# A batched f32 matmul with subtraction: x loaded as f16 through GpSimd's DMA queue into a ring of slots

## The chip, the cores and the metric

The kernel runs on one core of a Trainium2 chip. The metric is the device time of one execution in microseconds (us). The times shown are those of several executions of the kernel, with their median; one further execution was recorded by the hardware profiler and gives the profile and the trace.

A core has five engines with a queue of instructions each: TensorE (PE; its weight loads are listed apart as PEld), VectorE (DVE), ScalarE (ACT), GpSimd (POOL) and SyncE (SP). Transfers between the chip's DRAM and the core's memory (SBUF) are issued from such a queue and carried out by 16 DMA engines.

## The reference

```python
def setup_inputs():
    batch, m, k, n = 16, 512, 1024, 768
    return {
        "x": np.random.randn(batch, m, k).astype(np.float32),
        "weight": np.random.randn(k, n).astype(np.float32),
        "sub_value": np.random.randn(batch, m, n).astype(np.float32),
    }

def reference(x, weight, sub_value):
    return (np.matmul(x, weight) - sub_value).astype(np.float32)
```

Batch and m together are 8192 rows. x holds 33.55 MB, sub_value and the output 25.17 MB each, and weight 3.15 MB: 87.04 MB that must cross between DRAM and SBUF at least once.

## The kernel before

The 8192 rows are worked as 64 m tiles of 128 rows. Eight m tiles form a block whose rows are dealt so that each of the 128 partitions holds eight neighbouring rows of DRAM; a transfer of n neighbouring tiles therefore reads n rows in one piece for each partition (4 KB of x and 3 KB of sub_value or output per row).

For an m tile the steps are these. Its x rows, f32, are loaded (`load_x`, issued at L87). ScalarE casts them to f16 (`cast`, L108, or L105 for the tiles in `ON_DVE`). TensorE needs x with k on the partitions, so the tile is transposed. For 50 tiles TensorE does it, four times 128x128 words of 32 bits, each word a pair of f16 values (L116), into `psum_t`, and ScalarE copies the result to `xt_tile` (L123). For the 14 tiles of `ON_DVE`, taken in pairs, VectorE does it with 16 block transposes a pair (L137) into `xtp_tile`. Sixteen matmuls of 128x384 follow (L149): four chunks c of k, two interleaved halves r of each chunk, two halves of n. They accumulate in `psum_o`, of which there are three buffers. VectorE then subtracts (`finish`, L160): it reads `psum_o` and the tile of sub_value and writes the result over the latter. The output is stored from there (`store`, L97).

The weight comes in four chunks (L79) that pass through buffers of the sub_value pool and are cast to f16 by VectorE (L81).

All transfers are issued from SP in program order. The first 20 are listed in `HEAD_TRANSFERS`: single x tiles alternate with weight chunks, then single tiles of x and sub_value alternate, then pairs. From m tile 3 on the main loop issues, at every fourth tile, a group of four x tiles three groups ahead, a group of four sub_value tiles two groups ahead, and the store of the group two groups back. x has four buffers of four tiles, sub_value with output seven.

Every instruction is kept in program order on its engine (`keep`). In the main loop, TensorE's order is: the matmuls of chunk c of tile mi, then a transpose of tile mi + 2, and so on for four chunks. ScalarE casts four tiles ahead (seven for pairs of `ON_DVE`). At the start TensorE runs matmuls on zeros (`idle`) in the gaps while the first x tiles and the weight arrive; tiles 0 to 2 are multiplied chunk by chunk as the weight comes in.

Of the kernel before, what the change touches and what calls it, by code (L numbers as in the profile page):

```python
# [8 lines left out]
P = 128  # L9
Q = 32  # L10
F32 = mybir.dt.float32
F16 = mybir.dt.float16

S = 8
G = 4
XA, SA, OA = 3, 2, 2
TA = 2
CA = 2
LEAD_DVE = 7
PER = 4  # L20
HEAD = 3
ON_DVE = frozenset(range(18, 60, 6))
HEAD_TRANSFERS = [('x', 0, 1), ('w', 0, 0), ('x', 1, 1), ('w', 1, 0), ('x', 2, 1), ('w', 2, 0), ('w', 3, 0), ('x', 3, 1), ('s', 0, 1), ('x', 4, 1), ('s', 1, 1), ('x', 5, 1), ('s', 2, 1), ('x', 6, 1), ('s', 3, 1), ('x', 7, 1), ('x', 8, 2), ('s', 4, 2), ('x', 10, 2), ('s', 6, 2)]


@with_exitstack
def kernel(
# [7 lines left out]
    nc = tc.nc  # L35
    keep = tc.keep_in_program_order
# [5 lines left out]
    M_TOT, K = x_flat.shape  # L42
    _, N = weight.shape
    n_mt = M_TOT // P
    n_g = n_mt // G
    NS = N // 2
    KW = K // 2
    n_c = KW // P

    x_s = x_flat.rearrange("(s p j) k -> s p j k", p=P, j=S)  # L50
    sub_s = sub_flat.rearrange("(s p j) n -> s p j n", p=P, j=S)
    out_s = out_flat.rearrange("(s p j) n -> s p j n", p=P, j=S)
    w_c = weight.rearrange("(c p r) n -> c p r n", p=P, r=2)

    def rows(view, mi, n):
        return view[mi // S][:, mi % S : mi % S + n]

    const_pool = ctx.enter_context(tc.tile_pool(name="const", bufs=1))
    w_pool = ctx.enter_context(tc.tile_pool(name="w_pool", bufs=1))
    x_pool = ctx.enter_context(tc.tile_pool(name="x_pool", bufs=4))  # L60
    x16_pool = ctx.enter_context(tc.tile_pool(name="x16_pool", bufs=CA + 2))
    xt_pool = ctx.enter_context(tc.tile_pool(name="xt_pool", bufs=TA + 3))
    x16p_pool = ctx.enter_context(tc.tile_pool(name="x16p_pool", bufs=2))
    xtp_pool = ctx.enter_context(tc.tile_pool(name="xtp_pool", bufs=2))
    so_pool = ctx.enter_context(tc.tile_pool(name="so_pool", bufs=7))
    psum_t_pool = ctx.enter_context(tc.tile_pool(name="psum_t", bufs=2, space=bass.MemoryType.PSUM))
    psum_o_pool = ctx.enter_context(tc.tile_pool(name="psum_o", bufs=3, space=bass.MemoryType.PSUM))

# [3 lines left out]

    w_sb = w_pool.tile([P, n_c, 2, N], F16)

    x_t, so_t, x16_t, xt_t, ps_t, po_t = {}, {}, {}, {}, {}, {}

    def load_w(c):
        st = so_pool.tile([P, 2, N], F32, name="w_stage", tag="so_tile")
        keep(nc.sync.dma_start(out=st, in_=w_c[c]))  # L79
        for r in range(2):  # L80
            keep(nc.vector.tensor_copy(out=w_sb[:, c, r], in_=st[:, r]))  # L81

    def load_x(mi, n):
        g, j = divmod(mi, G)
        if j == 0:
            x_t[g] = x_pool.tile([P, G, K], F32, name="x_tile")
        keep(nc.sync.dma_start(out=x_t[g][:, j : j + n], in_=rows(x_s, mi, n)))  # L87

    def load_sub(mi, n):
        g, j = divmod(mi, G)  # L90
        if j == 0:
            so_t[g] = so_pool.tile([P, G, N], F32, name="so_tile")
        keep(nc.sync.dma_start(out=so_t[g][:, j : j + n], in_=rows(sub_s, mi, n)))

    def store(mi, n):
        g, j = divmod(mi, G)
        keep(nc.sync.dma_start(out=rows(out_s, mi, n), in_=so_t[g][:, j : j + n]))  # L97

    def cast(mi):
        g, j = divmod(mi, G)  # L100
        first = mi - mi % 2
        if first in ON_DVE:
            if mi == first:
                x16_t["pair", mi] = x16p_pool.tile([P, 2, K], F16, name="x16p_tile")
            keep(nc.scalar.copy(out=x16_t["pair", first][:, mi - first], in_=x_t[g][:, j]))  # L105
            return
        x16_t[mi] = x16_pool.tile([P, K], F16, name="x16_tile")
        keep(nc.scalar.copy(out=x16_t[mi], in_=x_t[g][:, j]))  # L108


    def transposes(mi):
        def one(c):
            def f():
                if c == 0:
                    ps_t[mi] = psum_t_pool.tile([P, K], F16, name="psum_t")
                keep(nc.tensor.transpose(  # L116
                    ps_t[mi].bitcast(F32)[:, c * P : (c + 1) * P],
                    x16_t[mi].bitcast(F32)[:, c * P : (c + 1) * P],
                    ident,
                ))  # L120
                if c == n_c - 1:
                    xt_t[mi] = xt_pool.tile([P, K], F16, name="xt_tile")
                    keep(nc.scalar.copy(out=xt_t[mi], in_=ps_t.pop(mi)))  # L123
                    x16_t.pop(mi)
            return f
        return [one(c) for c in range(n_c)]

    def transposes_dve(mi):

        x16 = x16_t.pop(("pair", mi)).bitcast(F32).rearrange("p j (c q) -> p (j c) q", c=n_c)  # L130
        xt_p = xtp_pool.tile([P, 2, K], F16, name="xtp_tile")
        xt_t[mi], xt_t[mi + 1] = xt_p[:, 0], xt_p[:, 1]
        xt = xt_p.bitcast(F32).rearrange("p j (c m) -> p (j c) m", c=n_c)

        def one(a, b):
            def f():
                keep(nc.vector.transpose(  # L137
                    xt[b * Q : (b + 1) * Q, :, a * Q : (a + 1) * Q],
                    x16[a * Q : (a + 1) * Q, :, b * Q : (b + 1) * Q],
                ))  # L140
            return f
        return [one(a, b) for a in range(P // Q) for b in range(P // Q)]

    def matmuls(mi, c):
        if c == 0:
            po_t[mi] = psum_o_pool.tile([P, 2, 512], F32, name="psum_o")
        for r in range(2):
            for h in range(2):
                keep(nc.tensor.matmul(  # L149
                    po_t[mi][:, h, :NS],  # L150
                    xt_t[mi][:, 2 * P * c + r : 2 * P * (c + 1) : 2],
                    w_sb[:, c, r, h * NS : (h + 1) * NS],
                    start=(c == 0 and r == 0),
                    stop=(c == n_c - 1 and r == 1),
                ))

    def finish(mi):
        g, j = divmod(mi, G)
        o = so_t[g][:, j].rearrange("p (h n) -> p h n", h=2)
        keep(nc.vector.tensor_tensor(  # L160
            out=o, in0=po_t.pop(mi)[:, :, :NS], in1=o, op=mybir.AluOpType.subtract
        ))


    for kind, at, n in HEAD_TRANSFERS:
        {"w": lambda: load_w(at), "x": lambda: load_x(at, n), "s": lambda: load_sub(at, n)}[kind]()


    idle_w = const_pool.tile([P, P], F16)
# [5 lines left out]
    def idle(n):  # L175
        for _ in range(n):
            keep(nc.tensor.matmul(idle_o[:, 0], idle_w, idle_x, start=True, stop=True))  # L177

    def lead(mi):
        return LEAD_DVE if mi - mi % 2 in ON_DVE else TA + CA  # L180

    def transpose_tile(mi):
        for f in transposes(mi):
            f()

    idle(13)
    cast(0)
    transpose_tile(0)
    idle(5)
    matmuls(0, 0)  # L190
    cast(1)
    transpose_tile(1)
    idle(4)
    matmuls(0, 1)
    matmuls(1, 0)
    matmuls(1, 1)
    cast(2)
    transpose_tile(2)
    idle(3)
    matmuls(0, 2)  # L200
    matmuls(1, 2)
    for c in range(3):
        matmuls(2, c)
    cast(3)
    transpose_tile(3)
    for mi in range(HEAD):
        matmuls(mi, 3)
        finish(mi)
    for mi in range(HEAD + 1, HEAD + TA):
        cast(mi)  # L210
        transpose_tile(mi)
    for mi in range(HEAD + TA, n_mt):
        if mi - lead(mi) < HEAD:
            cast(mi)


    waiting = []
    for mi in range(HEAD, n_mt):
        g, j = divmod(mi, G)
        if j == 0 or mi == HEAD:  # L220
            if g + XA < n_g:
                load_x((g + XA) * G, G)
            if g + SA < n_g:
                load_sub((g + SA) * G, G)
            if g >= OA:
                store((g - OA) * G, G)
        t = mi + TA
        tr = transposes(t) if t < n_mt and t - t % 2 not in ON_DVE else []
        for c in range(n_c):
            matmuls(mi, c)  # L230
            if tr:
                tr[c]()
        for t in range(mi, n_mt):
            if t - lead(t) == mi:
                cast(t)
        finish(mi)
        if mi + LEAD_DVE - 1 in ON_DVE:
            waiting += transposes_dve(mi + LEAD_DVE - 1)
        for f in waiting[:PER]:
            f()  # L240
        del waiting[:PER]
    for g in range(n_g - OA, n_g - 1):
        store(g * G, G)
    store(n_mt - G, G - 2)
    store(n_mt - 2, 1)
    store(n_mt - 1, 1)


# [28 lines left out]
```

## Time and profile before

| what | value |
|---|---|
| median of 8 executions | 213.08 us (212.73 to 213.47) |
| the profiled execution, its own time | 212.74 us |
| the profiled execution, span from the first to the last instruction | 211.0 us |
| granted TensorE clock, mean | 0.992 of full speed |
| DMA, mean over the span | 413 GB/s |
| L160, the subtraction | 64 times, 957 ns each |
| L123, the copy of a transposed tile | 50 times, 1012 ns each |
| L108 and L105, the casts of x | 50 times 1048 ns and 14 times 1046 ns |
| L137, VectorE's transposes | 112 times, 436 ns each |

The span lies within the execution's own time; 1.74 us of that execution are outside it. In the profile a line L123 is line 123 of the kernel. A group of instructions is shown as line, engine, operation, output <- input, shape and count, then the busy time in us, the mean of one in ns, and the idle time of the engine just before them with what ended most of it. In the row PEclk and the row DMA each digit is a tenth of full clock, or of the DMA engines' time, in one of 40 equal slices of the span. A line of the timeline or of the chain of waits starts with the start in us and the duration in us. A line of the windows has the stretch in us, its length, then busy time and count of instructions for PE, PEld, DVE, ACT and POOL, then the granted clock, the share of DMA time and GB/s.

### The profile page before, as it was taken

The page shows a single profiled execution, that of the slowest core. Times are in us where ns is not written, and L with a number is a line of the kernel's source. Part 1 is how long each engine was busy: PE and PEld are TensorE (multiplying, and loading weights), DVE is VectorE, ACT ScalarE, POOL GpSimd, SP SyncE. Part 2 cuts the span into 40 slices and gives each one's busy share as a digit, 9 for nine tenths or more (in the row PEclk, how much of TensorE's full clock was granted, in tenths as well). Part 3 has the DMA queues.
Part 4 walks back from the last instruction along what each step waited for, and adds up shares of the span by engine and source line. Part 5 has one row for each costly group of instructions (what it writes and reads, how often), then busy time and mean ns, then how long its engine had stood idle before and what let it go on. Part 6 is the DMA issues. An engine that isn't in the chain of part 4 may idle for free.

```text
span 211.0 us, 3028 instructions
## 1 busy us (share of the span) xinstructions
PE 198.5 (94%) x1249; PEld 130.0 (62%) x1249; DVE 114.0 (54%) x186; ACT 112.6 (53%) x115; POOL 0.7 (0%) x6
## 2 busy tenths in 40 slices
PE   7999799999999999999989999997999999999970
PEld 2465566677666666666656577664656766766640
DVE  0343313152597299389519939940993995133330
ACT  3646666757842847465086555508655552567300
POOL 1000000000000000000000000000000000000000
PEclk9999999999999999999999999999999999999996
DMA  6999999999999999999999999999999999999994
GB/s 225 423 409 400 419 418 430 440 415 432 425 416 433 424 422 430 444 415 434 419 431 426 425 436 411 435 422 428 434 423 434 418 436 423 422 426 424 433 409 170
DMA packets 9374, 87.23 MB, mean 413 GB/s; under 512 B 1040, under 2 KB 1040, under 8 KB 3728
## 3 DMA queue, kind: packets, MB, share of 16 engines
q1 hardware_dynamic: 9360, 87.04, 98.3%
q8 instruction: 10, 0.16, 0.3%
q14 instruction: 4, 0.03, 0.0%
HBM read 61.87 MB, written 25.17 MB: 413 GB/s over the span
## 4 chain that ended last, share of the span: by engine, by line
DMA 49%; PE 33%; ACT 9%; DVE 3%; SPq 1%; issue 1%; ACTq 0%
DMA x_tile<-in_x_dram 49%; PE psum_o L149 28%; PE psum_t L116 5%; ACT x_tile L108 4%; ACT xt_tile L123 3%; ACT x16p_tile L105 2%; DVE xtp_tile L137 2%; DVE so_tile L160 1%; SPq L79 1%; SPq L87 1%; ACTq L105 0%
## 5 line engine op out<-in xcount | busy, mean ns | idle before, releaser
L149 PE MATMUL psum_o<-w_sb,xt_tile 128*128 128x384 f16 x800 | 145.9, 326 | 2.1 <-ACT xt_tile L123 2.1
L149 PEld LDWEIGHTS <-xt_tile 128*128 128x128 f16 x800 | 78.2, 98 | 42.2 <-ACT xt_tile L123 3.2
L160 DVE TENSOR_TENSOR so_tile<-psum_o,so_tile 128x768 f32<-128x768 f32 x64 | 60.7, 957 | 57.3 <-PE psum_o L149 39.5
L123 ACT COPY xt_tile<-psum_t 128x1024 f16<-128x1024 f16 x50 | 50.6, 1012 | 59.7 <-PE psum_t L116 59.0
L137 DVE STREAM_TRANSPOSE xtp_tile<-x16p_tile 32x256 f32<-32x256 f32 x112 | 48.8, 436 | 22.8 <-ACT x16p_tile L105 21.0
L108 ACT CAST x_tile<-x_tile 128x1024 f16<-128x1024 f32 x50 | 51.7, 1048 | 6.7 <-DMA x_tile<-in_x_dram 6.7
L116 PE MATMUL psum_t<-ident,x_tile 128*128 128x128 f32 x200 | 52.4, 274 | 1.9 <-ACT x_tile L108 1.4
L149 PE MATMUL psum_o<-w_sb,xtp_tile 128*128 128x384 f16 x224 | 42.9, 326 | 0.6 <-DVE xtp_tile L137 0.6
L116 PEld LDWEIGHTS psum_t<-ident,x_tile 128*128 128x128 f32 x200 | 27.6, 141 | 16.0 <-ACT x_tile L108 4.3
L149 PEld LDWEIGHTS <-xtp_tile 128*128 128x128 f16 x224 | 21.8, 98 | 10.9 <-DVE xtp_tile L137 1.4
L105 ACT CAST x16p_tile<-x_tile 128x1024 f16<-128x1024 f32 x14 | 14.6, 1046 | 20.6 <-DMA x_tile<-in_x_dram 20.6
L81 DVE CAST w_sb<-w_stage 128x768 f16<-128x768 f32 x8 | 4.1, 556 | 10.5 <-DMA w_stage<-in_weight_dram 10.5
L177 PE MATMUL psum_o<-idle_x,idle_w 128*128 128x512 f16 x25 | 8.4, 491 | 1.3 <-DVE idle_x L172 1.3
L177 PEld LDWEIGHTS <-idle_w 128*128 128x128 f16 x25 | 3.1, 122 | 4.9 <-issue 3.2
L108 ACT ACT_TABLE_LOAD x1 | 1.3, 1283 | 0.7 <-PEq L261 0.7
L171 DVE MEMSET idle_w<- 128x64 uint32 x1 | 0.1, 112 | 0.8 <-PEq L261 0.8
masks.py:199 POOL TENSOR_SCALAR_AFFINE_SELECT ident<-ident 128x128 f32<-128x128 f32 x1 | 0.3, 292 | 0.1
L172 DVE MEMSET idle_x<- 128x256 uint32 x1 | 0.3, 272 | 0.0
masks.py:197 POOL MEMSET ident<- 128x128 f32 x1 | 0.2, 204 | 0.3 <-POOLq L261 0.3
L261 POOL MEMSET const-bfloat16-1.0<- 128x1 bf16 x1 | 0.1, 101 | 0.0
L261 POOL MEMSET const-uint8-127<- 128x1 uint8 x1 | 0.1, 101 | 0.0
L261 POOL MEMSET const-float32-0.0<- 128x1 f32 x1 | 0.1, 99 | 0.2 <-issue 0.2
(1 smaller groups left out, 0.1 us busy)
## 6 DMA issues: line engine op xcount, KB each, us to landing
x_tile<-in_x_dram SPq DMA_DIRECT2D x13, 2048.0 KB, 31.0
out_dram<-so_tile SPq DMA_DIRECT2D x15, 1536.0 KB, 31.9
so_tile<-in_sub_value_dram SPq DMA_DIRECT2D x14, 1536.0 KB, 33.1
x_tile<-in_x_dram SPq DMA_DIRECT2D x8, 512.0 KB, 10.5
w_stage<-in_weight_dram SPq DMA_DIRECT2D x4, 768.0 KB, 8.6
x_tile<-in_x_dram SPq DMA_DIRECT2D x2, 1024.0 KB, 12.8
so_tile<-in_sub_value_dram SPq DMA_DIRECT2D x4, 384.0 KB, 11.0
so_tile<-in_sub_value_dram SPq DMA_DIRECT2D x2, 768.0 KB, 13.4
```

Of the source, the lines that this page charges most:

```text
L79: keep(nc.sync.dma_start(out=st, in_=w_c[c]))
L81: keep(nc.vector.tensor_copy(out=w_sb[:, c, r], in_=st[:, r]))
L87: keep(nc.sync.dma_start(out=x_t[g][:, j : j + n], in_=rows(x_s, mi, n)))
L105: keep(nc.scalar.copy(out=x16_t["pair", first][:, mi - first], in_=x_t[g][:, j]))
L108: keep(nc.scalar.copy(out=x16_t[mi], in_=x_t[g][:, j]))
L116: keep(nc.tensor.transpose(ps_t[mi].bitcast(F32)[:, c * P : (c + 1) * P], x16_t[mi].bitcast(F32)[:, c * P : (c + 1) * P], ident,))
L123: keep(nc.scalar.copy(out=xt_t[mi], in_=ps_t.pop(mi)))
L137: keep(nc.vector.transpose(xt[b * Q : (b + 1) * Q, :, a * Q : (a + 1) * Q], x16[a * Q : (a + 1) * Q, :, b * Q : (b + 1) * Q],))
L149: keep(nc.tensor.matmul(po_t[mi][:, h, :NS], xt_t[mi][:, 2 * P * c + r : 2 * P * (c + 1) : 2], w_sb[:, c, r, h * NS : (h + 1) * NS], start ...
L160: keep(nc.vector.tensor_tensor(out=o, in0=po_t.pop(mi)[:, :, :NS], in1=o, op=mybir.AluOpType.subtract))
L177: keep(nc.tensor.matmul(idle_o[:, 0], idle_w, idle_x, start=True, stop=True))
L261: nc = _bacc.Bacc("TRN2", target_bir_lowering=False, num_devices=1)
```

## The change

The x buffers become one ring of 32 slots, one m tile of f16 each (`x_ring`). The buffers of sub_value and output become one ring of 32 slots of f32 (`so_ring`); the four weight chunks pass through its last eight slots. Transfers are listed by hand in `TRANSFERS`, one list for GpSimd's queue and one for SP's, and take up to eight m tiles each. GpSimd's queue has all of x: tiles 0 to 3 singly, tiles 4 to 7 together, then eight at a time. As source and destination differ in type, the DMA casts x to f16 on its way. SP's queue has the weight, then sub_value for tiles 0 to 15, and then alternately the store of a block of eight tiles and the load of the block of sub_value sixteen tiles further on.

`issue` is called whenever a tile of x has been read, or a tile of output finished. It emits the next transfers of each list as long as the slots that they need have been freed by earlier instructions; the order in each queue is that of its list. ScalarE's casts and their buffers are gone. TensorE's and VectorE's transposes read `x_ring` directly. The order of the work on TensorE and VectorE, the idle matmuls at the start, the transposed tiles' buffers and those of PSUM are as before. In the changed kernel the transposes of TensorE stand at L134, the copies at L141, VectorE's transposes at L157, and the subtraction at L184.

```diff
-G = 4
-XA, SA, OA = 3, 2, 2
+NX, NSO = 32, 32
-CA = 2
-HEAD_TRANSFERS = [('x', 0, 1), ('w', 0, 0), ('x', 1, 1), ('w', 1, 0), ('x', 2, 1), ('w', 2, 0), ('w', 3, 0), ('x', 3, 1), ('s', 0, 1), ('x', 4, 1), ('s', 1, 1), ('x', 5, 1), ('s', 2, 1), ('x', 6, 1), ('s', 3, 1), ('x', 7, 1), ('x', 8, 2), ('s', 4, 2), ('x', 10, 2), ('s', 6, 2)]
+
+TRANSFERS = {"pool": [
+    ('x', 0, 1), ('x', 1, 1), ('x', 2, 1), ('x', 3, 1), ('x', 4, 4), ('x', 8, 8),
+    ('x', 16, 8), ('x', 24, 8), ('x', 32, 8), ('x', 40, 8), ('x', 48, 8), ('x', 56, 8),
+], "sp": [
+    ('w', 0, 1), ('w', 1, 1), ('w', 2, 1), ('w', 3, 1), ('s', 0, 4), ('s', 4, 4),
+    ('s', 8, 8), ('o', 0, 8), ('s', 16, 8), ('o', 8, 8), ('s', 24, 8), ('o', 16, 8),
+    ('s', 32, 8), ('o', 24, 8), ('s', 40, 8), ('o', 32, 8), ('s', 48, 8), ('o', 40, 8),
+    ('s', 56, 8), ('o', 48, 8), ('o', 56, 4), ('o', 60, 2), ('o', 62, 1), ('o', 63, 1),
+]}
...
-    x_pool = ctx.enter_context(tc.tile_pool(name="x_pool", bufs=4))
-    x16_pool = ctx.enter_context(tc.tile_pool(name="x16_pool", bufs=CA + 2))
+    x_pool = ctx.enter_context(tc.tile_pool(name="x_pool", bufs=1))
...
-    so_pool = ctx.enter_context(tc.tile_pool(name="so_pool", bufs=7))
+    so_pool = ctx.enter_context(tc.tile_pool(name="so_pool", bufs=1))
...
+    x_ring = x_pool.tile([P, NX, K], F16)
+    so_ring = so_pool.tile([P, NSO, N], F32)
+    todo = {q: list(t) for q, t in TRANSFERS.items()}
+    done = {"w": set(), "x": set(), "s": set(), "o": set(), "read": set(), "finish": set()}
+
+    def issue():
+        for queue in todo.values():
+            issue_from(queue)
+
+    def issue_from(todo):
+        while todo:
+            kind, at, n = todo[0]
+            span = set(range(at, at + n))
+            old = {t - NX if kind == "x" else t - NSO for t in span}
+            need, by = {
+                "w": (set(), "o"),
+                "x": ({t for t in old if t >= 0}, "read"),
+                "s": ({t for t in old if t >= 0}, "o"),
+                "o": (span, "finish"),
+            }[kind]
+            if not need <= done[by]:
+                return
+            todo.pop(0)
+            done[kind] |= span
...
+            here = ring[:, at % size : at % size + n]
+            there = view[at // S][:, at % S : at % S + n]
+            if kind == "x":
+                keep(nc.gpsimd.dma_start(out=here, in_=there))
+            elif kind == "o":
+                keep(nc.sync.dma_start(out=there, in_=here))
+            else:
+                keep(nc.sync.dma_start(out=here, in_=there))
...
-                    x16_t[mi].bitcast(F32)[:, c * P : (c + 1) * P],
+                    x_ring[:, mi % NX].bitcast(F32)[:, c * P : (c + 1) * P],
...
+                    done["read"].add(mi)
+                    issue()
...
-        x16 = x16_t.pop(("pair", mi)).bitcast(F32).rearrange("p j (c q) -> p (j c) q", c=n_c)
+        x16 = x_ring[:, mi % NX : mi % NX + 2].bitcast(F32).rearrange("p j (c q) -> p (j c) q", c=n_c)
...
-        if j == 0 or mi == HEAD:
-            if g + XA < n_g:
-                load_x((g + XA) * G, G)
-            if g + SA < n_g:
-                load_sub((g + SA) * G, G)
-            if g >= OA:
-                store((g - OA) * G, G)
...
-        for t in range(mi, n_mt):
-            if t - lead(t) == mi:
-                cast(t)
```

More of the change, by code (lines that the diff above doesn't have):

```diff
@@ L44 @@
     n_mt = M_TOT // P
-    n_g = n_mt // G
     NS = N // 2
@@ L59 @@
     w_pool = ctx.enter_context(tc.tile_pool(name="w_pool", bufs=1))
-    x_pool = ctx.enter_context(tc.tile_pool(name="x_pool", bufs=4))
-    x16_pool = ctx.enter_context(tc.tile_pool(name="x16_pool", bufs=CA + 2))
+    x_pool = ctx.enter_context(tc.tile_pool(name="x_pool", bufs=1))
     xt_pool = ctx.enter_context(tc.tile_pool(name="xt_pool", bufs=TA + 3))
-    x16p_pool = ctx.enter_context(tc.tile_pool(name="x16p_pool", bufs=2))
     xtp_pool = ctx.enter_context(tc.tile_pool(name="xtp_pool", bufs=2))
-    so_pool = ctx.enter_context(tc.tile_pool(name="so_pool", bufs=7))
+    so_pool = ctx.enter_context(tc.tile_pool(name="so_pool", bufs=1))
     psum_t_pool = ctx.enter_context(tc.tile_pool(name="psum_t", bufs=2, space=bass.MemoryType.PSUM))
@@ L73 @@
     w_sb = w_pool.tile([P, n_c, 2, N], F16)
[L75 to L108, printed above, removed]
+    x_ring = x_pool.tile([P, NX, K], F16)
@@ new lines @@
+    so_ring = so_pool.tile([P, NSO, N], F32)
+    xt_t, ps_t, po_t = {}, {}, {}
+    todo = {q: list(t) for q, t in TRANSFERS.items()}
[18 more added lines that the diff above has]
+            done[kind] |= span
+            if kind == "w":
+                first = NSO - 2 * (n_c - at)
+                st = so_ring[:, first : first + 2]
+                keep(nc.sync.dma_start(out=st, in_=w_c[at]))
+                for r in range(2):
+                    keep(nc.vector.tensor_copy(out=w_sb[:, at, r], in_=st[:, r]))
+                continue
+            ring, size, view = {
+                "x": (x_ring, NX, x_s), "s": (so_ring, NSO, sub_s), "o": (so_ring, NSO, out_s)
+            }[kind]
+            here = ring[:, at % size : at % size + n]
[6 more added lines that the diff above has]
+                keep(nc.sync.dma_start(out=here, in_=there))
@@ L114, in f @@
                 if c == 0:
+                    assert mi in done["x"]
                     ps_t[mi] = psum_t_pool.tile([P, K], F16, name="psum_t")
@@ L123, in f @@
                     keep(nc.scalar.copy(out=xt_t[mi], in_=ps_t.pop(mi)))
-                    x16_t.pop(mi)
+                    done["read"].add(mi)
+                    issue()
             return f
@@ L128, in transposes_dve @@
     def transposes_dve(mi):
-        x16 = x16_t.pop(("pair", mi)).bitcast(F32).rearrange("p j (c q) -> p (j c) q", c=n_c)
+        assert {mi, mi + 1} <= done["x"]
+        x16 = x_ring[:, mi % NX : mi % NX + 2].bitcast(F32).rearrange("p j (c q) -> p (j c) q", c=n_c)
         xt_p = xtp_pool.tile([P, 2, K], F16, name="xtp_tile")
@@ L140, in f @@
                 ))
+                if a == b == P // Q - 1:
+                    done["read"] |= {mi, mi + 1}
+                    issue()
             return f
@@ L157, in finish @@
     def finish(mi):
-        g, j = divmod(mi, G)
-        o = so_t[g][:, j].rearrange("p (h n) -> p h n", h=2)
+        assert mi in done["s"]
+        done["finish"].add(mi)
+        o = so_ring[:, mi % NSO].rearrange("p (h n) -> p h n", h=2)
         keep(nc.vector.tensor_tensor(
@@ L162, in finish @@
         ))
-    for kind, at, n in HEAD_TRANSFERS:
-        {"w": lambda: load_w(at), "x": lambda: load_x(at, n), "s": lambda: load_sub(at, n)}[kind]()
+        issue()
+    issue()
     idle_w = const_pool.tile([P, P], F16)
@@ L177, in idle @@
             keep(nc.tensor.matmul(idle_o[:, 0], idle_w, idle_x, start=True, stop=True))
-    def lead(mi):
-        return LEAD_DVE if mi - mi % 2 in ON_DVE else TA + CA
     def transpose_tile(mi):
@@ L186 @@
     idle(13)
-    cast(0)
     transpose_tile(0)
@@ L190 @@
     matmuls(0, 0)
-    cast(1)
     transpose_tile(1)
@@ L196 @@
     matmuls(1, 1)
-    cast(2)
     transpose_tile(2)
@@ L203 @@
         matmuls(2, c)
-    cast(3)
     transpose_tile(3)
@@ L209 @@
     for mi in range(HEAD + 1, HEAD + TA):
-        cast(mi)
         transpose_tile(mi)
-    for mi in range(HEAD + TA, n_mt):
-        if mi - lead(mi) < HEAD:
-            cast(mi)
     waiting = []
     for mi in range(HEAD, n_mt):
-        g, j = divmod(mi, G)
-        if j == 0 or mi == HEAD:
-            if g + XA < n_g:
-                load_x((g + XA) * G, G)
-            if g + SA < n_g:
-                load_sub((g + SA) * G, G)
-            if g >= OA:
-                store((g - OA) * G, G)
         t = mi + TA
@@ L241 @@
         del waiting[:PER]
[L242 to L246, printed above, removed]
+    assert not any(todo.values())
 _INS = ['x', 'weight', 'sub_value']
```

## The prediction

> **What bounds the kernel now.** I read the busy times first, then the 40 slices and the DMA queues, then the waits, and last the timeline of the start and the chain of waits. The page:
>
> ```profile
> PE 198.5 (94%) x1249; PEld 130.0 (62%) x1249; DVE 114.0 (54%) x186; ACT 112.6 (53%) x115; POOL 0.7 (0%) x6
> PEclk9999999999999999999999999999999999999996
> DMA  6999999999999999999999999999999999999994
> q1 hardware_dynamic: 9360, 87.04, 98.3%
> L149 PE MATMUL psum_o<-w_sb,xt_tile 128*128 128x384 f16 x800 | 145.9, 326 | 2.1 <-ACT xt_tile L123 2.1
> ```
>
> Two resources are full at once. The DMA engines are busy 98.3% of 211.0 us with 87.04 MB, all from one queue, and TensorE is busy 94% of it. ScalarE and VectorE have half their time free.
>
> The rate of TensorE can be read off the chain of waits, where it runs freely; stretches of three windows follow it:
>
> ```profile
> 31.11 0.11 PE psum_t L116
> 31.22 0.65 PE psum_o L149 x4
> 31.87 0.11 PE psum_t L116
> 31.98 0.65 PE psum_o L149 x4
> ```
> ```profile
> 0.00:31.87 31.87, 28.88 (x159) 16.75 (x160) 9.38 (x16) 17.98 (x18) 0.70 (x6) 1.00 0.96 383
> 31.87:204.45 172.58, 169.63 (x1093) 113.28 (x1090) 103.70 (x170) 94.60 (x98) 0.00 (x0) 1.00 1.01 427
> 204.45:211.00 6.55, 0.00 (x0) 0.00 (x0) 0.96 (x1) 0.00 (x0) 0.00 (x0) 0.72 0.52 213
> ```
>
> Four matmuls and one transpose come every 0.76 us, so a tile takes 4 x 0.76 = 3.04 us, and 4 x 0.65 = 2.6 us where VectorE transposes. With 50 tiles of the first kind and 14 of the second that is 188.4 us, 2.95 us a tile. From 31.87 us to the last matmul at 204.45 us TensorE stands still only 172.58 - 169.63 = 2.95 us. The DMA in that window moves 427 GB/s. An m tile is 0.524 MB of x, 0.393 MB of sub and 0.393 MB of out, 1.31 MB or 3.07 us: the same as TensorE's. So any lateness of TensorE in the start is kept to the end, and any DMA byte that becomes dearer lengthens the kernel.
>
> The timeline of the start shows when the first loads are used:
>
> ```profile
> 6.57 1.03 DVE L81 CAST w_sb<-w_stage 128x768 f16<-128x768 f32 x2 [5.36 <-DMA w_stage<-in_weight_dram]
> 14.76 1.03 DVE L81 CAST w_sb<-w_stage 128x768 f16<-128x768 f32 x2 [0.86 <-DMA w_stage<-in_weight_dram]
> 16.04 1.04 ACT L108 CAST x_tile<-x_tile 128x1024 f16<-128x1024 f32 x1 [1.98 <-DMA x_tile<-in_x_dram]
> ```
>
> The transfers are listed x0, w0, x1, w1, x2, w2, w3, x3, with 0.524 MB for an x tile and 0.786 MB for a w chunk. w0 has landed after 1.31 MB, w3 after 4.72, x3 after 5.24: (16.04 - 6.57) / (5.24 - 1.31) = 2.41 us per MB (0.415 MB/us), from 3.4 us on. What is listed first lands first. The transposes of tiles 5, 6, 7 and 8 begin at 22.54, 25.80, 28.84 and 31.87 us in the chain, each right behind the matmuls before it: x is in time there, because tiles 4 to 7 are single transfers and 8 to 11 pairs.
>
> **What the Trainium skill says.** "DMA: Bandwidth & Descriptors", section "SWDGE vs HWDGE vs iDMA": a cast in a DMA can be had only from GpSimd; "Issuing engines are not separate DMA queues": both queues run on the same 16 DMA engines. So a second queue gives no bandwidth; the trace agrees in so far as one queue fills them. The same page, "Queues, rings and completion order": a DMA engine takes the queues in turn, packet by packet. No run shows it yet. "SBUF — State Buffer", section "SBUF: two separate sides": a VectorE operation that uses its second port pair keeps GpSimd from writing descriptors. The candidates are eight w casts (L81, 4.1 us in all), so at most 4.1 us of descriptor writing, early. No page prices a cast.
>
> **The change part by part.**
>
> 1. ScalarE's casts go: 50 x 1.048 + 14 x 1.046 = 67 us of an engine at 53%. TensorE's waits for the cast copy are 4.3 + 1.4 us, mostly in the first 22 us, and after 31.87 us it loses 2.95 us, to late copies on ScalarE and late VectorE transposes behind it. I count 2.4 us gained: 0.70 + 0.30 + 1.38 at 108, 120 and 145 us, where the timeline has a wait for L123 or L137. At most 4 us, with a cast's delay in the start.
>
> 2. The x bytes. DMA reads the same 33.55 MB of f32 and writes half. Before, reads and writes of a transfer are equal in size, so the trace can't say which side binds. If the write side does, an x byte costs 0.5; if the read side, 1; if the cast has a rate of its own, more, and 2 is the upper bound that I keep. I take 1: every byte must still be read through engines that stand at 427 GB/s. Total then 87.04 / 0.427 = 204 us, as before: no gain and no loss in capacity.
>
> 3. The start. x4 to x7 become one transfer, x8 to x15 one of 4.19 MB, with one completion each; the changed program lets tile 8's first transpose wait for the whole of it. SP's queue holds w and sub 0 to 15 (9.44 MB) in the same time, with nothing to hold it back, as its first wait is that of the store of tiles 0 to 7, for L184 of tile 7. x8 to x15 are there when 8.39 MB of x are. If the queues share equally, 16.8 MB must move: 3.4 + 16.8 / 0.426 = 42.8 us. If SP's packets win (a sub row is up to 24 KB in one piece, a row of an x tile 4 KB), 17.8 MB: 45.3 us. I take 44.0 us against 31.87 us: TensorE stops for what adds up to **12.1 us**. Lateness ahead of it (x4 to x7, sub 0 to 3) is covered by this one, as TensorE waits for tile 8 anyway. So is GpSimd's issue: x0 comes behind the identity's 0.3 us (masks.py:199) and, by the skill's page ("Specifications"), some 0.4 us later to its first byte than on SP.
>
> 4. The middle. On SP the load of sub i+16 stands behind the store of tiles i to i+7, which waits for L184 of tile i+7; a pair is 6.29 MB and must be done in 8 x 2.95 = 23.6 us. x stays issued without a break: 25.2 MB remain at 44 us, and the ring is not full before its end. With equal shares SP gets 0.213 MB/us and a pair takes 29.5 us. From tile 7's finish at 44.0 + 6.6 = 50.6 us, subs 16, 24, 32 land at 80.1, 109.6, 139.1; they are needed at 77.2, 100.8, 124.4 by L184, plus 4.9 us that two spare psum_o buffers give: 3.9 us lost at tile 24, another 5.9 at tile 32; then x is through (156 us) and SP has all. Sum 9.8. If SP's packets win, x is the late one: a cycle of eight tiles is 10.48 MB, 24.6 us against 23.6, six cycles, 6 us. I take **8 us**; bounds 0 (a share just between) and 14 (x has 0.6).
>
> 5. The end: the last two stores are unchanged, so the 6.55 us behind the last matmul stay. SP's 65 issues, some 0.42 us each in the start's timeline (1.16 us: w0), become 24, with 12 on GpSimd, hidden beside transfers on both sides.
>
> Sum: +12.1 - 2.4 + 8 = +17.7 us. Against the profiled execution (212.74 us, 1.74 around the span of 211.0) 230.4; against the median of 213.08, 230.8. **I forecast 231 us.**
>
> **The rivals.**
>
> A. *The cast halves x's cost in the DMA.* For it: the writes halve. Against: reads don't. Total 70.3 MB, 165 us, so TensorE alone bounds. Place: the start. With x at 0.4 of the engines' time, x8 to x15 are there at 3.4 + 4.19 / 0.4 / 0.42 = 28.3 us, in time, and sub 0 to 3 at 3.4 + 4.72 / 0.6 / 0.42 = 22.1, some 1.2 us late for the psum_o buffer of tile 3. 213.1 + 1.2 - 2.4 = 211.9, with the cast's delay in the start gone about 211: not slower. It decides from an x byte at about 0.6 downward: at 0.7, 5.87 / 0.4 / 0.42 puts x8 at 38.3 us and 6 us are lost. With equal shares at 0.5 sub 0 to 3 come at about 26 us and the kernel is at 216.
>
> B. *The cast is slow in the DMA.* For it: the conversion is work the engines don't do now, and x comes in 2 KB rows per tile. Against: nothing in the trace. At 1.5 the load is 103.8 MB-equivalents: 3.4 + 103.8 / 0.427 = 246.5, with the last tiles and the end 255 us; at 2, 120.6 and 295 us.
>
> C. *One long stall only.* The shares fall so that the middle costs nothing: 213.1 + 12.1 - 2.4 = 223 us. It differs from the forecast only in step 4.
>
> That the rings make false waits is a rival that I drop: the changed program's waits are per transfer and per tile.
>
> **How the numbers follow.** Forecast (x byte at 0.9 to 1.15; 225 to 240 us) 0.47; C 0.12; B 0.28; A 0.13, of which 0.08 ends below the time before, 0.02 at it and 0.03 above. The range: A's slower part and its loss at 0.7 sit near 216, so it starts there; B reaches it up to about 1.55, so I end at 266. Outside stay about 0.1 below and 0.1 above. What can be told from no change is about 0.2%, 0.4 us. Faster 0.08, same 0.02, slower 0.90.
>
> **What would show it.** Step 3: L134 on TensorE with one wait of about 10 us or more for the DMA into x_ring before 46 us. Step 4: L184 idle for the DMA of sub near tiles 24 and 32, or L134 for x at each eighth tile. Step 2: GpSimd's queue with about 38% of the engines' time; a far larger share means B, about 24% means A. The forecast is wrong if x8 to x15 land before 33 us, or if the DMA no longer holds near 426 GB/s, counted as f32, between 10 and 40 us.

## The result and the profile after

The changed kernel takes 239.24 us (median of 11 runs, 237.15 to 240.26) against 212.99 us (median of 32 runs of the kernel before beside it). The ratio is 1.1215, with a 95% interval of 1.1194 to 1.1236: slower by 12%, where 231 us had been forecast. The profiled execution has a span of 237.0 us against 211.0.

The page of the changed kernel, with the rows that answer to those of before:

```profile
PE 204.6 (86%) x1249; PEld 133.7 (56%) x1249; DVE 113.4 (48%) x186; ACT 51.9 (22%) x51; POOL 7.3 (3%) x18
PEclk9779955999999996599999999999999999999999
DMA  6999999999999999999999999994974399347363
q1 hardware_dynamic: 3456, 53.48, 54.2%
q0 software_dynamic: 1728, 16.78, 33.7%
```

Three things are to be seen. First, the DMA engines are full for the first 27 slices, about 160 us, and then half idle: early on TensorE waits for transfers, later the transfers wait for TensorE. Second, x now counts with the 16.78 MB that are written, but it takes 33.7% of 237.0 us, 79.9 us; against the 33.55 MB that are read that is 420 GB/s. SP's queue moves 53.48 MB in 54.2%, 128.5 us, or 416 GB/s. Third, the TensorE clock has dips that it did not have before.

The timeline of TensorE, every row with a wait for a DMA or a subtraction of more than 2 us after the first x tile (start, duration; in brackets the idle time before it and what ended it):

```profile
36.44 1.12 PE L134 MATMUL psum_t<-ident,x_ring 128*128 128x128 f32 x4 [9.97 <-DMA x_ring<-in_x_dram]
96.22 1.44 PE L172 MATMUL psum_o<-w_sb,xtp_tile 128*128 128x384 f16 x4 [8.45 <-DVE so_ring L184]
```

The first row is the transpose of tile 4; the transposes of tile 8 that follow wait for nothing: x8 to x15 have landed at 45.5 us, and TensorE comes to them at 49.65. The second is tile 19, which needs the `psum_o` buffer of tile 16, whose subtraction came late for want of sub. VectorE's waits for sub, in its own timeline:

```profile
95.21 2.69 DVE L184 TENSOR_TENSOR so_ring<-psum_o,so_ring 128x768 f32<-128x768 f32 x3 [12.97 <-DMA so_ring<-in_sub_value_dram]
119.88 0.96 DVE L184 TENSOR_TENSOR so_ring<-psum_o,so_ring 128x768 f32<-128x768 f32 x1 [6.08 <-DMA so_ring<-in_sub_value_dram]
145.48 0.96 DVE L184 TENSOR_TENSOR so_ring<-psum_o,so_ring 128x768 f32<-128x768 f32 x1 [5.57 <-DMA so_ring<-in_sub_value_dram]
```

These are tiles 16, 24 and 32, each the first of a block of eight. A subtraction is the best mark of progress, as there is one for each tile. Its start in us, from VectorE's timeline of the two kernels:

| tile | 3 | 7 | 16 | 24 | 32 | 63 | end of span |
|---|---|---|---|---|---|---|---|
| before | 25.1 | 37.2 | 65.7 | 87.1 | 114.7 | 204.45 | 211.0 |
| after | 43.0 | 55.2 | 95.2 | 119.9 | 145.5 | 232.83 | 237.0 |

Up to tile 7 the change costs 17.95 us, from tile 7 to tile 63 10.4 us (177.66 against 167.23), and behind tile 63 it gains 2.4 us (4.17 against 6.55, as the last store finds the DMA free). The sum is 26.0 us, the difference of the spans.

### The profile page after: what moved, and what is told of

The parts are those of the page before. It is cut to its first block, busy times and chain, and to the rows that moved or that the text cites. A ratio compares the mean times of both kernels' runs of the same rounds, so it can differ in the third digit from the quotient of the medians.

```text
span 237.0 us, 2904 instructions
## 1 busy us (share of the span) xinstructions
PE 204.6 (86%) x1249; PEld 133.7 (56%) x1249; DVE 113.4 (48%) x186; ACT 51.9 (22%) x51; POOL 7.3 (3%) x18
## 3 DMA queue, kind: packets, MB, share of 16 engines
q1 hardware_dynamic: 3456, 53.48, 54.2%
q0 software_dynamic: 1728, 16.78, 33.7%
## 4 chain that ended last, share of the span: by engine, by line
PE 49%; DMA 43%; DVE 4%; POOL 1%; issue 0%; SPq 0%; POOLq 0%; DVEq 0%
PE psum_o L172 44%; DMA so_ring<-in_sub_value_dram 29%; DMA x_ring<-in_x_dram 14%; PE psum_t L134 6%; DVE so_ring L184 2%; DVE xtp_tile L157 1%; POOL x_ring L121 1%; SPq L123 0%; POOL ident masks.py:199 0%; POOL ident masks.py:197 0%; DVEq L184 0%; POOLq masks.py:199 0%; POOLq L258 0%
## 5 line engine op out<-in xcount | busy, mean ns | idle before, releaser
L172 PE MATMUL psum_o<-w_sb,xt_tile 128*128 128x384 f16 x800 | 148.9, 331 | 0.6 <-DVE so_ring L184 0.6
L184 DVE TENSOR_TENSOR so_ring<-psum_o,so_ring 128x768 f32<-128x768 f32 x64 | 60.7, 957 | 107.8 <-PE psum_o L172 82.9
L172 PEld LDWEIGHTS <-xt_tile 128*128 128x128 f16 x800 | 79.3, 99 | 41.7 <-issue 3.1
L141 ACT COPY xt_tile<-psum_t 128x1024 f16<-128x1024 f16 x50 | 50.6, 1012 | 176.1 <-PE psum_t L134 176.1
L134 PE MATMUL psum_t<-ident,x_ring 128*128 128x128 f32 x200 | 54.3, 285 | 15.2 <-DMA x_ring<-in_x_dram 15.2
L172 PE MATMUL psum_o<-w_sb,xtp_tile 128*128 128x384 f16 x224 | 45.1, 337 | 11.1 <-DVE so_ring L184 8.5
L157 DVE STREAM_TRANSPOSE xtp_tile<-x_ring 32x256 f32<-32x256 f32 x112 | 48.7, 435 | 1.7
L134 PEld LDWEIGHTS psum_t<-ident,x_ring 128*128 128x128 f32 x200 | 29.0, 148 | 29.3 <-DMA x_ring<-in_x_dram 11.6
L121 POOL DMA_DIRECT2D x_ring<-in_x_dram x12 | 6.6, 570 | 124.1 <-PE psum_t L134 101.0
L200 PE MATMUL psum_o<-idle_x,idle_w 128*128 128x512 f16 x25 | 9.0, 516 | 1.3 <-DVE idle_x L195 1.3
L113 DVE CAST w_sb<-so_ring 128x768 f16<-128x768 f32 x8 | 4.1, 558 | 10.0 <-DMA so_ring<-in_weight_dram 10.0
```

The source lines that it names most:

```text
L113: keep(nc.vector.tensor_copy(out=w_sb[:, at, r], in_=st[:, r]))
L121: keep(nc.gpsimd.dma_start(out=here, in_=there))
L134: keep(nc.tensor.transpose(ps_t[mi].bitcast(F32)[:, c * P : (c + 1) * P], x_ring[:, mi % NX].bitcast(F32)[:, c * P : (c + 1) * P], ident,))
L157: keep(nc.vector.transpose(xt[b * Q : (b + 1) * Q, :, a * Q : (a + 1) * Q], x16[a * Q : (a + 1) * Q, :, b * Q : (b + 1) * Q],))
L172: keep(nc.tensor.matmul(po_t[mi][:, h, :NS], xt_t[mi][:, 2 * P * c + r : 2 * P * (c + 1) : 2], w_sb[:, c, r, h * NS : (h + 1) * NS], start ...
L184: keep(nc.vector.tensor_tensor(out=o, in0=po_t.pop(mi)[:, :, :NS], in1=o, op=mybir.AluOpType.subtract))
```

## The experiments

**Packet size in the middle: e1 and e2.** Each x transfer of eight tiles from tile 16 on is cut into two, or into four, as here:

```diff
-    ('x', 16, 8), ('x', 24, 8), ('x', 32, 8), ('x', 40, 8), ('x', 48, 8), ('x', 56, 8),
+    ('x', 16, 4), ('x', 20, 4), ('x', 24, 4), ('x', 28, 4), ('x', 32, 4), ('x', 36, 4),
+    ('x', 40, 4), ('x', 44, 4), ('x', 48, 4), ('x', 52, 4), ('x', 56, 4), ('x', 60, 4),
```

> From tile 16 on x comes in transfers of four tiles (16 KB of source per packet) in place of eight (32 KB); all else as in the changed kernel. Theory: the DMA engines take the two queues in turn, a packet at a time, so a queue's share follows from its packet's size: x had 32/(32+24) = 0.57 beside sub and out, and gets 16/(16+24) = 0.40. The store of tiles 0 to 7 and sub 16 to 23 (6.29 MB) then take about 25 us in place of 38.6, tile 16's subtraction no longer waits 13 us, and the time falls by some 10 us, to about 228. Rival: the queues share equally in bytes, or GpSimd's queue is favoured as such: tile 16 still waits for sub until about 95 us, and the time stays at 237 to 240.

> From tile 16 on x in transfers of two tiles (8 KB of source per packet). Theory of packets in turn: x gets 8/(8+24) = 0.25 beside sub and out, the store of tiles 0 to 7 with sub 16 to 23 takes about 20 us, no wait for sub at tile 16; x may now become the late one in the middle. Time 225 to 232. Rival (shares don't depend on the packet): sub 16 to 23 still take some 38 us and the time stays at 237 to 240.

Measured: 226.8 us (ratio 1.0655, 1.0613 to 1.0698), as expected, and 222.37 us (1.0447, 1.041 to 1.0484), below the range expected. The size of x's transfers in the middle, and with it that of their packets, decides about 12 and 17 us. One line of windows for each kernel, from the issue of the store of tiles 0 to 7 on (stretch, length, busy times, clock, DMA share, GB/s): first the changed kernel, then e1, then e2.

```profile
57.00:95.00 38.00, 30.77 (x201) 20.94 (x200) 14.54 (x24) 9.11 (x9) 0.53 (x1) 0.94 1.00 299
```
```profile
55.00:84.00 29.00, 29.00 (x191) 19.80 (x189) 14.54 (x24) 8.10 (x8) 1.58 (x3) 1.00 1.02 326
```
```profile
54.00:78.00 24.00, 24.00 (x160) 16.77 (x159) 12.49 (x21) 7.80 (x9) 2.11 (x4) 1.00 1.03 345
```

The last number rises from kernel to kernel: x counts in it with half of what it costs, so SP's queue moves more. It gives no share by itself, as SP's queue moves nothing in the first 3 us or so of each stretch. The packets' own times in the three traces give it. What the profile calls a packet is here one partition's row: the 24 transfers on SP make 3456 packets and the 12 on GpSimd 1728, 144 for each, that is one for each of the 128 partitions and 16 of 4 bytes. The Trainium skill, "DMA: Bandwidth & Descriptors", section "Queues, rings and completion order", says that a DMA engine goes from queue to queue after each packet. The traces agree: while SP moves the 256 packets of the store of tiles 0 to 7 and of sub 16 to 23, x moves 253 in the changed kernel (261 beside 265 in e1, 299 beside 256 in e2). The median packet of 24 KB took 0.925 us, that of x 1.226, 0.624 or 0.322 us (32, 16 or 8 KB). Each of the 16 engines has 16 of SP's packets to move and, in turn, as many of x's between them:

| x packet | 16 x (SP's packet + x's packet) | measured, first to last packet | x's share in turn |
|---|---|---|---|
| 32 KB | 34.4 us | 33.8 us (59.9 to 93.6) | 0.57 |
| 16 KB, e1 | 24.8 us | 25.1 us (58.1 to 83.2) | 0.40 |
| 8 KB, e2 | 20.0 us | 20.6 us (57.6 to 78.2) | 0.26 |

The rival, equal shares in bytes whatever the packet, falls. In e2 TensorE has no wait for a DMA or a subtraction after 35.75 us.

**The start: e3.** Sub 4 to 15 go from SP's list to GpSimd's, behind the x tiles that are needed sooner:

```diff
-    ('x', 4, 4), ('x', 8, 8),
+    ('x', 4, 4), ('s', 4, 4), ('x', 8, 8), ('s', 8, 8),
...
-    ('s', 0, 4), ('s', 4, 4), ('s', 8, 8), ('o', 0, 8),
+    ('s', 0, 4), ('o', 0, 8),
```

> Sub 4 to 15 move from SP's list to GpSimd's, behind x4 to x7 and behind x8 to x15; all else as in the changed kernel. Theory: x4 to x7 were late because SP's 9.44 MB went ahead of most of it; now only 8.9 MB (w, sub 0 to 3, x0 to x7) are before their end: 3.4 + 8.9/0.42 = 24.6 us in place of 36.4, and TensorE's low clock after the long stop goes too. Time lower by 12 to 15 us, about 225; the wait for sub 16 remains. Rival: the start is late because GpSimd's queue starts slowly or the cast is slow (x0 used at 10.2 us against 4.7): then x3 to x7 come hardly earlier and the gain is under 4 us.

Measured: 238.24 us (1.1193, 1.1146 to 1.1239). The cause of the late start is confirmed: x4 to x7, landed at 24.5 us, no longer stop TensorE, and tile 7 is subtracted at 47.3 us in place of 55.2. The gain at the end was not as expected: it is none. Three stops show where it went, in the timeline of TensorE in e3 (L130 are the transposes here, L168 the matmuls, L180 the subtraction):

```profile
39.31 0.45 PE L130 MATMUL psum_t<-ident,x_ring 128*128 128x128 f32 x1 [3.88 <-DMA x_ring<-in_x_dram]
88.42 1.44 PE L168 MATMUL psum_o<-w_sb,xtp_tile 128*128 128x384 f16 x4 [8.53 <-DVE so_ring L180]
122.70 1.44 PE L168 MATMUL psum_o<-w_sb,xt_tile 128*128 128x384 f16 x4 [8.93 <-DVE so_ring L180]
```

The first is tile 8: with x4 to x7 in time it is x8 to x15 (landed at 38.9 us) that TensorE waits for, as the forecast had it, and the granted clock is 0.50 until 44.3 us. The third stop is new, and tile 24 comes at 121.7 us, against 119.9 with the late start. The middle has a pace of its own: the arrival of sub on SP's queue.

**TensorE's clock: e9.** 40 matmuls on zeros into a `psum_t` buffer stand in the wait for x4 to x7:

```diff
+    fill = psum_t_pool.tile([P, K], F16, name="psum_t")
+    for _ in range(40):
+        keep(nc.tensor.matmul(fill.bitcast(F32), idle_w, idle_x, start=True, stop=True))
     for mi in range(HEAD + 1, HEAD + TA):
         transpose_tile(mi)
```

> The changed kernel with 40 matmuls on zeros in TensorE's wait for x4 to x7 (about 8.5 us of work in a wait of 10). Theory: TensorE ran at half clock for 5.6 us after that wait because it had stood still; busy, it keeps its clock, and the finish of tile 7 comes at 52 to 53 us in place of 55.2, the end about 3 us sooner. Rival: the low clock has another reason, or the end is bound by sub in the middle whatever the start: finish of tile 7 at 55, or the end unchanged at 237 to 240.

Measured: 239.56 us (1.125, 1.1181 to 1.1319). The same stretch in the windows of the changed kernel, then of e9; the last number but two is the granted clock:

```profile
38.00:40.00 2.00, 2.00 (x8) 1.18 (x7) 0.00 (x0) 0.60 (x1) 0.00 (x0) 0.50 1.21 270
```
```profile
38.00:40.00 2.00, 2.00 (x15) 1.39 (x14) 0.00 (x0) 0.27 (x1) 0.00 (x0) 1.00 1.18 258
```

With TensorE kept busy, the clock is full and nearly twice the instructions are done; tile 7 comes at 52.3 us, 2.8 us sooner, as expected. The end is where it was, as in e3 and as the rival had it: tile 24 comes at 122.0 us.

**One part alone: e4, e7 and e8.** All three are the kernel before, with its transfers at their old places. In e4 x goes to GpSimd's queue with the cast; in e8 it goes there uncast; in e7 everything is in GpSimd's one queue, x cast. In the edit, the lines that drop ScalarE's casts (e4, e7) and that move w, sub and the stores to GpSimd (e7) are left out.

```diff
-            x_t[g] = x_pool.tile([P, G, K], F32, name="x_tile")
-        keep(nc.sync.dma_start(out=x_t[g][:, j : j + n], in_=rows(x_s, mi, n)))
+            x_t[g] = x_pool.tile([P, G, K], F16, name="x_tile")      # e4, e7
+        keep(nc.gpsimd.dma_start(out=x_t[g][:, j : j + n], in_=rows(x_s, mi, n)))      # e4, e7, e8
...
```

> The kernel before with one thing of the change: each x load is issued by GpSimd at its place and cast to f16 by the DMA into the same tile buffers, and ScalarE's casts are gone. Theory: the cast costs the DMA nothing beside a plain copy of the f32 bytes, and what is lost is the order of x against w at the start (x tiles of 4 KB packets beside w of 6 KB): 214 to 222 us. Rival: the cast itself is dear for the DMA: over 225 us. Other rival: the queue beside SP's and the freed ScalarE are a gain by themselves: below 212.5.

> The kernel before in its own order, with every transfer issued by GpSimd in one queue, x cast by the DMA and ScalarE's casts gone. Theory: the cast costs the DMA nothing and it is the second queue that breaks the order of arrival: with one queue the order is back, 211 to 214 us. Rival: what cost 4 us in the kernel before with x on GpSimd's queue is the cast or GpSimd's making of descriptors: 215 us or more.

> The kernel before with x issued by GpSimd, uncast, into the f32 buffers; ScalarE casts as before. Theory: two queues are the cost, with or without a cast: 215 to 219 us, as with the cast (216.8), and the late x at the start again. Rival (the cast is the cost): 212.5 to 213.5 us.

| | x uncast, cast by ScalarE | x cast by the DMA |
|---|---|---|
| one queue | before, SP's: 212.7 us | e7, GpSimd's: 215.93 us (ratio 1.0142, 1.0115 to 1.0169) |
| two queues | e8: 218.57 us (1.0262, 1.023 to 1.0294) | e4: 216.81 us (1.0188, 1.0161 to 1.0215) |

e4 and e8 are in their ranges. With two queues the cast in the DMA, with ScalarE's casts gone, is 1.8 us better than none, so it isn't what costs. A second queue costs 5.9 us without the cast. e7 is above its expectation, and its number alone would speak for the rival. Its timeline of VectorE says otherwise (L150 is the subtraction):

```profile
200.46 0.96 DVE L150 TENSOR_TENSOR so_tile<-psum_o,so_tile 128x768 f32<-128x768 f32 x1 [1.64 <-PE psum_o L139]
```

The last tile comes 4.0 us sooner than before, the earliest of all these runs. The loss is behind it. The windows of e7's end, then two lines of the kernel before:

```profile
200.00:205.00 5.00, 0.42 (x3) 0.03 (x1) 0.96 (x1) 0.00 (x0) 0.54 (x1) 0.94 0.99 420
205.00:208.00 3.00, 0.00 (x0) 0.00 (x0) 0.00 (x0) 0.00 (x0) 0.00 (x0) 0.50 0.83 344
208.00:211.00 3.00, 0.00 (x0) 0.00 (x0) 0.00 (x0) 0.00 (x0) 0.00 (x0) 0.50 0.13 55
211.00:214.30 3.30, 0.00 (x0) 0.00 (x0) 0.00 (x0) 0.00 (x0) 0.00 (x0) 0.50 0.00 0
```
```profile
208.00:210.00 2.00, 0.00 (x0) 0.00 (x0) 0.00 (x0) 0.00 (x0) 0.00 (x0) 0.50 0.18 72
210.00:211.00 1.00, 0.00 (x0) 0.00 (x0) 0.00 (x0) 0.00 (x0) 0.00 (x0) 0.50 0.00 0
```

The DMA is busy to about 208 us whatever TensorE does: that is the 87 MB. It also starts later, with the first packet at 2.8 us in place of 1.7, as GpSimd's first issue comes at 1.45 us, behind the identity, in place of 0.74 on SP. Then 3.3 us of the span are empty; in the kernel before it is 1 us.

**Looking for a better kernel: e5, e6, e10, e11 and e12.** e5 joins e3 and e2.

```diff
-    ('x', 4, 4), ('x', 8, 8), ('x', 16, 8),
+    ('x', 4, 4), ('s', 4, 4), ('x', 8, 2), ('x', 10, 2), ('x', 12, 2), ('x', 14, 2), ('s', 8, 8),
+    ('x', 16, 2), ('x', 18, 2), ('x', 20, 2), ('x', 22, 2),
...
```

> Both edits together: sub 4 to 15 behind x4 and x8 on GpSimd's list, and x from tile 8 on in transfers of two tiles. Alone the first moved the finish of tile 7 forward by 7.9 us and gained nothing at the end, the second left no stop of TensorE after 36 us (222.4 us). Theory: the first one's gain was given back because the middle was bound by SP's share of the packets; with that gone it stays: 222.4 - 8 = about 214 to 215 us. Rival: the gain of the start is lost in the middle for another reason (the bytes of the DMA as a whole): 219 to 222 us.

Measured: 219.63 us (1.0305, 1.0274 to 1.0336): the rival's value. VectorE now waits for x up to 10.4 us with its transposes, the subtractions stand behind these, and tile 13 is subtracted only at 69.3 us. The tiles that it waits for, x18 and x19, come in small packets, behind sub 8 to 15 in GpSimd's list.

e6 has x, weight and sub in one list on GpSimd's queue, in the order of the kernel before, and the stores alone on SP.

```diff
+TRANSFERS = {"pool": [
+    ('x', 0, 1), ('w', 0, 1), ('x', 1, 1), ('w', 1, 1), ('x', 2, 1), ('w', 2, 1), ('w', 3, 1), ('x', 3, 1),
...
+    ('x', 16, 4), ('s', 12, 4), ('x', 20, 4), ('s', 16, 4), ('x', 24, 4), ('s', 20, 4),
...
+], "sp": [
+    ('o', 0, 4), ('o', 4, 4), ('o', 8, 4), ('o', 12, 4),
...
+    ('o', 56, 4), ('o', 60, 2), ('o', 62, 1), ('o', 63, 1),
+]}
```

> x, weight and sub in one list on GpSimd's queue, in the order and sizes of the kernel before at the start, then four tiles each; SP's queue has the stores alone, in blocks of four. Theory: as the cast costs the DMA nothing and the order of the start is restored, what is left is the DMA's own floor of 3.4 + 87.04/0.426 = 207.7 us and the last store: 209 to 212 us, about the kernel before or 1% under it. Rival: descriptors of all loads made by GpSimd are a limit, or the start of its queue costs several us: 214 to 220 us.

Measured: 219.78 us (1.0329, 1.0314 to 1.0345), 8 us above the range of the theory and in that of the rival. The start is good (tile 3 at 25.7 us), but the first store goes out at 26.7 us and takes packets from the loads: tile 8 waits for its sub until 51.3 us, against 43.7 before and 44.5 in e7, where GpSimd issues the loads too and the stores stand in the same queue.

The last three start from e7 and give some stores to SP: e10 those of the last four groups, e11 all, e12 those of the last two groups.

```diff
+        eng = nc.sync if g >= 12 else nc.gpsimd      # e10; e11: always nc.sync; e12: g >= 14
+        keep(eng.dma_start(out=rows(out_s, mi, n), in_=so_t[g][:, j : j + n]))
```

> As e7_one_queue_cast (one queue on GpSimd in the order of the kernel before, x cast), but the stores of the last four groups, which are issued when all loads but the last few are under way, go to SP. Theory: e7's TensorE ended at 200.5 us against 204.4, and what it lost lay behind it: the DMA worked until 208.4 us and the span went on to 214.3 behind the last DMAs of GpSimd's queue. With SP's queue last, the end comes some 1 to 2 us behind the DMA's floor: 209.5 to 211.5 us, faster than before by 0.5 to 1.5%. Rival: the 6 us at the end belong to any kernel that uses GpSimd's queue, whoever issues last: 214 to 216 us.

> As e7, but all stores go to SP, at their places in the program of the kernel before. Theory: a store on a queue of its own no longer stands behind loads that were issued earlier but takes its turn packet by packet, so sub and x come later in the middle: slower than e10 by several us, 213 to 218 us. Rival: the order among loads and stores doesn't matter as long as the loads have one queue: within 1 us of e10.

> As e10, but only the stores of the last two groups (tiles 56 to 63) go to SP; they are issued from about 190 us on, when every load has landed, so they can overtake nothing but a store. Theory: e10 was slow because its SP stores, from 169 us on, took packets from the loads of the last tiles (TensorE stood still at 188.6 us for x, and tile 56's sub came at 193.5 us); without that TensorE ends at about 200.5 us as in e7, the DMA at its floor of 208.4 us, and the end is behind it by 1 to 2 us: 210 to 212 us, faster than before by up to 1%. Rival: the 6 us behind the DMA's end in e7 come with GpSimd's queue as such: 214 to 216 us.

Measured: e10 216.03 us (1.0144, 1.0107 to 1.0181), e11 220.09 us (1.0335, 1.0308 to 1.0363), e12 214.37 us (1.0073, 1.0059 to 1.0087). e10 missed, at the rival's upper end but for another cause: its stores overtook the loads of the last tiles (tile 56's subtraction at 193.5 us against 184.8 in e7). e11 is 4 us slower than e10, and above its range; like e6 it shows that stores with a turn of their own reach the DMA too soon. e12 does what was meant, the last tile at 200.71 us, and yet is 0.7% slower than the kernel before: the rival's value. Its end in the windows:

```profile
205.00:208.00 3.00, 0.00 (x0) 0.00 (x0) 0.00 (x0) 0.00 (x0) 0.00 (x0) 0.50 0.85 346
208.00:210.00 2.00, 0.00 (x0) 0.00 (x0) 0.00 (x0) 0.00 (x0) 0.00 (x0) 0.50 0.15 60
210.00:212.60 2.60, 0.00 (x0) 0.00 (x0) 0.00 (x0) 0.00 (x0) 0.00 (x0) 0.50 0.01 4
```

The DMA finishes no sooner than in the kernel before (last packet at 210.4 us, against 209.7), although the tiles finish 3.7 us sooner, and some 2 us behind it are empty. What holds up the end here and in e7 is GpSimd's closing DRAIN, an instruction behind the last line of each of these kernels; the other engines wait for it before they end. e7 and e12, from the view of the kernel's last line (count, shortest, middle and longest in ns, first and last start):

```profile
L262 POOLq DRAIN  x3: 46/90/11914, 201.7 to 214.1; - x3
L263 POOLq DRAIN  x3: 46/96/33548, 178.3 to 212.3; - x3
```

The long one of each is the first. It ends at 213.6 and 211.8 us, 3.1 and 2.9 us behind the last packet of GpSimd's queue (210.5 and 208.9), while SP is through with its waits for landings at 211.1 and 210.8: 2.5 and 1.0 us are lost by it. In e10 that queue is empty at 204.5 us and the DRAIN ends at 207.3, before the stores do; there the span ends 1.3 us behind the last packet, as in the kernel before. Over the kernels with GpSimd's queue this time behind its last packet grows with the number of transfers that it issued: 0.9 us with 12 (the changed kernel), 1.6 with 30 (e2), 2.4 with 47 (e6), 3.1 with 65 (e7). Why it does is open, and so is what would have come of e7's order with fewer and larger transfers. None of the twelve kernels beats the kernel before.

## Why the prediction was right or wrong

The direction and the range were right, and the sum was 8 us short. That it came so near is in part luck: its terms came out differently from what they were named after, and e3 shows that the two large ones are not added.

*Step 1, ScalarE's casts.* 2.4 us were put down. e7, which differs from the kernel before in the cast and the queue, ends its tiles 4.0 us sooner; that fits a gain, but no run has GpSimd's one queue without the cast, so what the casts' share is stays unshown. In the changed kernel it can't be seen.

*Step 2, an x byte costs the DMA as much as a plain f32 byte.* Right: 420 GB/s of source against 416 on SP's queue, 32 KB of x in 1.226 us on a DMA engine against 24 KB in 0.925 on SP's queue (26.7 and 26.6 GB/s), and e4 against e8 shows no loss from the cast. Rivals A (half the cost) and B (one and a half) fall.

*Step 3, the start.* This is the step that failed. It gave 12.1 us and had x8 to x15 as the late transfer, with the lateness of x4 to x7 "covered by this one". The reverse held: x4 to x7 stopped TensorE until 36.44 us against 19.84 before, and x8 to x15 were in time. Their landing was forecast well (44.0 us, measured 45.5); but 13.2 us of work lie between the transposes of tiles 4 and 8, so after the first stop TensorE came to tile 8 only at 49.65 us. The variant in which SP's packets win was worked out for x8 to x15 alone; the same sum for x4 to x7 is 3.4 + (9.44 + 4.19) / 0.42 = 35.9 us, close to what was measured. The start cost 17.95 us at tile 7, 5.9 more than forecast; about half of the excess, 2.8 us, is TensorE's half clock after the stop (e9). GpSimd's slower first byte, put down as some 0.4 us, was more: 4.15 us from the first issue to x's first packet (1.41 to 5.56), against 1.03 on SP (0.74 to 1.77) and 1.38 in e7, where GpSimd's queue is alone. Why it is so long beside SP's queue is open.

*Step 4, the middle.* The mechanism was right, x's large packets keeping sub from SP's queue, and e1 and e2 show it. The equal shares of the first sum were too kind: x had 0.57, a pair of store and load took 33.8 us in place of 29.5, and TensorE's stop came with tile 16, not with 24 and 32. The other sum gave SP the larger packets, from the 4 KB row of a single x tile; a transfer of eight x tiles has 32 KB in one piece, which is more than the 24 KB of sub. From tile 7 on 8 less 2.4 us were put down, and 10.4 measured. Rival C, a middle that costs nothing, falls.

That 12.1 and 8 were *added* was wrong in form. e3 and e9 gain 7.9 and 2.8 us at tile 7 and nothing at the end. The table shows it, with the start of the subtraction in us:

| tile | 7 | 24 | 63 |
|---|---|---|---|
| after | 55.2 | 119.9 | 232.8 |
| e3, start mended | 47.3 | 121.7 | 231.9 |
| e9, clock kept | 52.3 | 122.0 | 232.1 |
| e2, small x packets | 53.1 | 103.0 | 216.3 |

Tile 24 needs w, sub 0 to 31 and the stores of tiles 0 to 15, 22.0 MB, from SP's list. The DMA is full from 3.4 to 120 us and moves 0.42 x 116.6 = 49 MB in that time; by subtraction x had some 27 MB, 52 tiles, when tile 24 was due (27.7 MB by the trace's packets). The ring of 32 slots lets x run that far ahead, and its packets make it do so. So the order of arrival, not the start, sets the pace up to tile 32; from there to the end TensorE runs at its own rate (87.3 us for 31 tiles, against 89.7 before).

*Step 5, the end.* It was to stay at 6.55 us; it fell to 4.17 because the DMA is half idle by then.

The forecast's 231 us against 239.24: 5.9 us too little for the start, 4.8 too little from tile 7 on, 2.4 too much behind tile 63, which makes 8.3.

## What to carry to other kernels

Where one queue keeps the DMA full, its list is also the order of arrival. A second queue gave no bandwidth in these runs; each queue got a share by the size of its packets, and what was listed late could overtake what was needed soon. A deep ring should make that worse for whoever shares the DMA with it, though no run here varies its depth. Work out what each queue has moved by the time that a given tile is due, and do so for every transfer that this tile waits for, not only for the largest. And two stops that hang on the same stream of bytes are not added: the first one's cure may only make the second one longer.

## What was not expected of the hardware

- After waits of 4.23, 9.97 and 8.45 us TensorE's granted clock was 0.50, for 4.9, 6.1 and 4.3 us of the work that followed (to 15.2, 42.5 and 100.5 us); 40 matmuls on zeros in the second of these waits kept it at 1.00 (e9).
- A cast from f32 to f16 in the DMA ran at 420 GB/s of source bytes, no slower than plain transfers beside it (416).
- Two queues shared the DMA engines packet for packet, even with a whole row of 32 KB as a packet: 6.29 MB on SP's queue took 33.8, 25.1 and 20.6 us beside x packets of 32, 16 and 8 KB.
- GpSimd's closing DRAIN ended 0.9 us behind the last packet of its queue with 12 transfers issued and 3.1 us with 65 (the changed kernel, e7), and held up the end of e7 and e12.
